# A four-mixer transformer stack in f32: first norm from rows, a clock guard, and two program parts recorded in turn

## The chip, the cores and the metric

The kernel runs on one core of one Trainium2 chip. The metric is device time in microseconds (us) of one execution, the median of several. Engines are named as the profile does: PE is TensorE (PEld its weight loads), DVE is VectorE, ACT is ScalarE, POOL is GpSimd, SP is the engine that issues most transfers. A "product" below is one matrix multiplication instruction of PE.

## The reference

A sequence of 512 rows of width 1024 passes four layers; each is a mixer and then a gated feed-forward part of hidden width 2816, both behind an RMS norm, and a last RMS norm closes the stack. Everything is float32.

```python
def rmsnorm(x, g):
    y = x * rsqrt(mean(square(x), -1) + 1e-5)
    return y * g

def rwkv7_mix(x, ...):                       # layer 0: 16 heads of 64
    xx = token_shift(x) - x
    xr, xw, xk, xv, xa, xg = (x + xx * mu[c] for c in range(6))
    r, k, v = xr @ w_r, xk @ w_k, xv @ w_v
    ...                                      # decay d, gates a and g, normalized key kk
    def step(state, t):                      # 512 steps of a 64 x 64 state per head
        sa = state @ kk_t
        state = state * d_t - outer(sa, kk_t * a_t) + outer(v_t, k_t)
        return state, state @ r_t
    ...                                      # group norm of y, a bonus term, gate, output product

h = x
for i, mix in enumerate((rwkv7_mix, swa_sink_mix, sgu_chunk_mix, gla_mix)):
    h = h + mix(rmsnorm(h, norm_mix[i]))
    h = h + (silu(n @ w_gate) * (n @ w_up)) @ w_out        # n = rmsnorm(h, norm_ffn[i])
return rmsnorm(h, norm_final)
```

The second mixer is attention in a window of 128 with a sink, the third a gated unit with chunks of 128, the fourth gated linear attention.

## The kernel before

The host passes x twice: `x`, with the 512 tokens in rows, and `x_t`, with the 1024 features in rows (eight tiles of 128 features x 512 tokens).

**The planner.** The code does not issue instructions directly: class `K` records operations into a `Program`, and `Program.run` (a list scheduler) issues them. Among the next `WINDOW` = 700 recorded operations it always takes the one that can start first by its own prices (`price`), and among equals the one recorded first. Recording order therefore sets priorities and which buffers are taken, but not alone the order on an engine. Each engine then executes its own instructions strictly in the order that was issued. All operations are recorded by one helper, so the profile gives the line L233 for all of them; groups are told apart by tile names.

**Fills.** The planner models PE's clock: it counts product columns per stretch of `TICK` = 3413 ns, and takes PE at half speed where the stretch before had less than `BUSY`. `keep_warm` puts products of the 128 x 128 identity with itself ("fills", their own line L448) where it expects PE to wait at least `GAP` = 450 ns. A fill writes to a PSUM bank that nobody reads.

**Weights.** A large product in f32 is split in three: `weights` loads a tile `wraw`, ACT copies it to a rounded `whi`, DVE (or, with `pool` true, POOL) subtracts to get `wlo`; `mm3` multiplies hi by hi, hi by lo and lo by hi.

**The mix stage** (`rwkv`). The first norm: ACT squares the eight tiles of `x_t`, DVE adds them up (`acc`), PE transposes, DVE reduces to one mean per token (`ms`), `rsqrt` makes `rcol` in ten small operations, PE broadcasts it along features by transposes, DVE copies it out of PSUM (`rbc`, a tile `slot`). Then, for each of the eight feature tiles, DVE multiplies `h` by gain and `rbc`, forms the shifted difference `xx`, and mixes; the products of the key follow with `rw_w_k`, whose `wlo` POOL makes for the first four tiles.

**The groups.** The sixteen heads are worked off in four groups. `ahead(n)` prepares group n: `rwkv_prepare` (elementwise, a scan `ew`, tiles `et`, `qk`), two halves of `rwkv_products` (`pa`, `pr`), `rwkv_inverse` (an inverse of 64 x 64 triangles by a ping-pong of products on PE and masked sums on DVE, tiles `mt` and `iv`; two parts), `rwkv_direct`. `rwkv_chain` then walks group n through the eight blocks of 64 tokens (four loops of two, the state in `st`, tiles `vu`, `wu`), with `rwkv_out` after every second loop (tiles `out`, `grs`, partly on POOL). The state makes the chain a strict sequence. In the program the whole of `ahead(n + 1)` is recorded, then the whole of chain n. `ahead(0)` comes first; the product of v (`gemm_tok`) fills the time beside it.

**Attention** (`swa`, `attend`): scores from 64-row products, the maximum on DVE (`mx`), exponentials on ACT, the scaling by POOL (`slot<-slot,smx`), transposes on PE, and products with the values; weight products of the neighbouring projections stand among them.

**The end** (`finish`, `store`): DVE multiplies the sums by the final gain, `rcol` is made for each half, ACT and DVE scale one half tile each, and SP issues eight transfers of 256 KB.

Of the kernel before, what the change touches and what calls it, by code (L numbers as in the profile page):

```python
# [29 lines left out]
ALSO = {"exp": ("tanh",), "sigmoid": ("tanh",), "silu": ("sin", "tanh"), "gelu": ("tanh",)}  # L30
ORDER = 1
EARLY = (("pa", 1), ("iv", 4), ("ew", 4))
# [157 lines left out]
class Program:  # L190
# [5 lines left out]
    FREE, GAP, TAIL, TURN = 4, 450.0, 150.0, 92.0  # L196
    TICK, BUSY = 10240 / 3, 3350.0

    def __init__(self, tc):
        self.tc, self.ops, self.last = tc, [], None  # L200
        nc = tc.nc
        self.tensor, self.vector, self.scalar = Engine(self, "PE", nc.tensor), Engine(self, "DVE", nc.vector), Engine(self, "ACT", nc.scalar)
        self.gpsimd, self.sync = Engine(self, "POOL", nc.gpsimd), Engine(self, "SP", nc.sync)
        self.cold, self.warm, self.fills, self.form = 0.0, None, 0, (P, P, 0)

    def pool(self, name, bufs, **kw):
# [81 lines left out]
    def run(self):  # L288
# [15 lines left out]
        while order < n:  # L304
# [40 lines left out]
            if e == "PE" and self.warm and op.ready > 0.0:  # L345
                now["PE"] = self.keep_warm(now["PE"], s, work)
                if now["PE"] > s:
                    continue
# [47 lines left out]
    def keep_warm(self, now, s, work):  # L396
# [7 lines left out]
        while True:  # L404
# [8 lines left out]
            now = t  # L413

    def count(self, work, span, t, cost, columns):
        n = int(t // span)
# [15 lines left out]
class K:  # L432
# [46 lines left out]
    def load_x(self, h):  # L479
        for k in range(KT):  # L480
            self.nc.sync.dma_start(h[k], self.d['x_t'][k * P:(k + 1) * P, :])

# [109 lines left out]
    def finish(self, half, nh):  # L592

        nc = self.nc
        c = slice(nh * S, nh * S + S)
        bs = (2 * half, 2 * half + 1)
        for b in bs:
            sq = self.slot()
            nc.scalar.activation(sq, self.h[b][:, c], AF.Square, accum_out=self.ss[:, 2 * b + nh:2 * b + nh + 1])
        if self.kind == 'final':  # L600
            for b in bs:
                nc.vector.tensor_mul(self.h[b][:, c], self.h[b][:, c], self.g[nh])
            return
# [71 lines left out]

    def rstd(self, acc=None):

        nc = self.nc
        if acc is None:
            col = self.rcol()  # L680
        else:
            ms, col = [self.sm.tile([P, NB], F32, name=n) for n in ("ms", "rcol")]
            ps = self.bank()
            for b in range(NB):
                nc.tensor.transpose(ps[:, b * P:(b + 1) * P], acc[:, b * P:(b + 1) * P], self.ident)
            nc.vector.tensor_reduce(ms, self.blocks(ps), axis=AX.X, op=ALU.add)
            nc.vector.tensor_scalar(ms, ms, 1.0 / D, EPS, op0=ALU.mult, op1=ALU.add)
            self.rsqrt(col, ms)
        ps = self.bank()
        for b in range(NB):  # L690
            nc.tensor.transpose(ps[:, b * P:(b + 1) * P], col[:, b:b + 1].to_broadcast([P, P]), self.ident)
        bc = self.slot()
        nc.vector.tensor_copy(bc, ps)
        return col, bc

# [220 lines left out]
    def rwkv(self, g, g_next, slots):  # L916
# [4 lines left out]

        nc, d, v = self.nc, self.d, self.v
        ex, inner, early, wide, tall = [ExitStack() for _ in range(5)]
# [10 lines left out]

        hn = self.h
        nc.vector.memset(keep, 1.0)
# [4 lines left out]
        acc = self.slot()  # L941
        for k in range(KT):
            t = acc if k == 0 else tp.tile([P, S], F32, name="t")
            nc.scalar.activation(t, hn[k], AF.Square)
            if k:
                nc.vector.tensor_add(acc, acc, t)
        _, rbc = self.rstd(acc=acc)
        xx = []
# [77 lines left out]
        def ahead(n):  # L1026
# [7 lines left out]
            subs.append(sb)  # L1034
            self.rwkv_prepare(sb, rf, kf, twa, keep, sel, rs, ka1)
            for hf in range(2):
                self.rwkv_products(sb, hf)
            self.rwkv_inverse(sb)
            self.rwkv_direct(sb)
        ahead(0)  # L1040
        for c in range(2):
# [48 lines left out]
    def rwkv_prepare(self, sb, rf, kf, twa, keep, sel, rs, ka1):  # L1090
# [18 lines left out]
        for i, p in enumerate(sb['pairs']):  # L1109
# [26 lines left out]
            nc.vector.tensor_mul(outer(qk), nat(rf[p]), nat(e))  # L1136
            sb['kn'].append(kn)
        ps = self.bank()
        for i in range(G):
# [26 lines left out]
    def rwkv_inverse(self, sb):  # L1166
# [29 lines left out]
        part = lambda t, r, j: t[r, j * 64:(j + 1) * 64]  # L1196
        sb['inv'] = []
        for k in range(2):
            zk = lambda r, j: z[r, k * 2048 + j * 256 + (64 if r.start else P):][:, :64]
# [3 lines left out]
            for lv in range(2):  # L1203
# [18 lines left out]
                u = u2  # L1222
            sb['inv'].append(u)

    def rwkv_direct(self, sb):
# [20 lines left out]
    def rwkv_chain(self, sb, tg):  # L1246
# [11 lines left out]
        for b in range(NB):  # L1258
# [46 lines left out]
            if b % 2:  # L1305
                self.rwkv_out(sb, b // 2, y, tg)

    def rwkv_out(self, sb, hf, y, tg):
# [460 lines left out]
def trace(prog, d, es, stages):  # L1769
    k = K(prog, d, es)  # L1770
    k.h = k.eight()
    k.load_x(k.h)
    k.v = k.load_cols()
    g_mix = lambda i: (lambda j: k.v['norm_mix'](i * KT + j))
# [42 lines left out]
```

## Time and profile before

| what | value |
|---|---|
| median of 3 runs | 2604.38 us (2601.57 to 2606.51) |
| the profiled execution's own time | 2596.65 us |
| its span | 2595.0 us, mean granted PE clock 0.994 |
| PE busy | 2517.9 us |
| DVE, ACT, POOL busy | 1802.4, 1314.1, 377.6 us |
| fills | 190 |
| first real product | 24.36 us |
| output products of the mix stage start | 461.28 us |

The span is that of one execution recorded by the profiler; the time beside it contains 1.65 us around the span. In a timeline row the columns are start, length, engine, line, operation, output and inputs, shape, count, and in brackets the engine's idle time ahead of it with what ended that. Adjacent alike instructions share a row. PE keeps two records of 0.27 us for one f32 fill, overlapped, so a count of 46 there is 23 fills. In a windows row the columns are the stretch, its length, busy time and instructions of PE, PEld, DVE, ACT and POOL, PE's granted clock (1.00 is full), the share of the transfer engines in use, and GB/s. A fill counts as busy PE.

### The profile page before, as it was taken

How to read it: one execution, taken by the hardware profiler on the slowest of the kernel's cores; microseconds unless marked ns; L12 is line 12 of the kernel's file. 1: busy time of each engine (PE TensorE's matmuls, PEld its weight loads, DVE VectorE, ACT ScalarE, POOL GpSimd, SP SyncE). 2: the span in 40 equal slices, each digit the busy share in tenths (PEclk: the TensorE clock that was granted, in tenths of full speed). 3: DMA queues.
4: the chain of work that ended last, by engine and by line, in shares of the span. 5: the costliest groups of instructions: out<-in, count | busy, mean ns of one | idle time of the engine just before them, and what ended most of it. 6: DMA issues, size and time to landing. Idle time of an engine off the chain costs nothing.

```text
span 2595.0 us, 37573 instructions
## 1 busy us (share of the span) xinstructions
PE 2517.9 (97%) x14378; PEld 2052.6 (79%) x14378; DVE 1802.4 (69%) x2804; ACT 1314.1 (51%) x2156; POOL 377.6 (15%) x521
## 2 busy tenths in 40 slices
PE   9999898999999989999999999999999999999998
PEld 8577777997888756988787888888878777888886
DVE  8685875487778863787776655577868634577868
ACT  4544454465646455656464333565556523565555
POOL 1000111022112232121221000012111000121111
PEclk9999999999999999999999999999999999999999
DMA  3220001489898412898985232389887221489885
GB/s 128 62 75 10 10 4 59 120 195 225 214 225 176 129 49 49 179 211 225 213 218 146 90 98 83 82 216 228 208 213 187 84 81 57 98 219 226 221 199 117
DMA packets 126004, 365.20 MB, mean 141 GB/s; under 512 B 13296, under 2 KB 19952, under 8 KB 125824
## 3 DMA queue, kind: packets, MB, share of 16 engines
q0 software_dynamic: 41472, 138.43, 29.8%
q1 hardware_dynamic: 84352, 224.37, 26.9%
q8 instruction: 113, 1.85, 0.3%
q14 instruction: 67, 0.55, 0.1%
HBM read 358.29 MB, written 2.10 MB: 139 GB/s over the span
## 4 chain that ended last, share of the span: by engine, by line
PE 47%; DMA 5%; issue 5%; DVE 4%; ACT 3%; POOL 0%; SPq 0%; ACTq 0%; POOLq 0%; DVEq 0%
PE ps L233 47%; DMA wraw<-ffn_w_b 3%; DVE slot L233 2%; ACT slot L233 2%; DMA wraw<-ffn_o_a 2%; DVE wlo L233 1%; ACT whi L233 1%; DMA wraw<-ffn_w_a 1%; DVE h L233 0%; POOL wraw L233 0%; DVE mx L233 0%; DMA slot<-slot 0%; SPq L233 0%; DVE left L233 0%; ACT left L233 0%
## 5 line engine op out<-in xcount | busy, mean ns | idle before, releaser
L233 PE MATMUL ps<-whi,slot 128*128 128x512 f32 (+1 forms) x5072 | 1557.7, 384 | 17.8 <-DVE slot L233 9.3
L233 PEld LDWEIGHTS ps<-whi,slot 128*128 128x128 f32 x5072 | 943.7, 188 | 199.5 <-issue 21.4
L233 DVE TENSOR_TENSOR wlo<-wraw,whi 128x1024 fp32r<-128x1024 f32 (+2 forms) x628 | 720.2, 1153 | 398.8 <-ACT whi L233 396.4
L233 ACT CAST whi<-wraw 128x1024 fp32r<-128x1024 f32 (+3 forms) x632 | 625.1, 993 | 732.2 <-PE ps L233 554.7
L233 PE MATMUL ps<-wlo,slot 128*128 128x512 f32 (+1 forms) x2536 | 969.1, 383 | 1.9 <-DVE wlo L233 1.7
L233 PEld LDWEIGHTS ps<-wlo,slot 128*128 128x128 f32 x2536 | 476.9, 188 | 86.1 <-DVE wlo L233 6.2
L233 PE MATMUL ps<-slot,whi 128*128 128x512 f32 (+2 forms) x864 | 275.8, 397 | 0.1
L233 DVE TENSOR_TENSOR slot<-ps,slot 128x512 f32<-128x512 f32 (+2 forms) x287 | 155.0, 566 | 91.0 <-PE ps L233 61.7
L233 PEld LDWEIGHTS ps<-slot,whi 128*128 128x128 f32 (+2 forms) x864 | 157.2, 185 | 48.3 <-issue 6.6
L233 POOL DMA_DIRECT2D wraw<-ffn_w_a x128 | 109.1, 853 | 512.5 <-DVE wlo L233 375.7
L233 PE MATMUL ps<-slot,wlo 128*128 128x512 f32 (+2 forms) x432 | 169.5, 393 | 0.8 <-DVE wlo L233 0.8
L233 POOL DMA_DIRECT2D wraw<-ffn_w_b x64 | 54.7, 859 | 772.7 <-DMA wraw<-ffn_w_b 517.8
L233 DVE TENSOR_TENSOR slot<-left,slot 128x512 fp32r<-128x512 f32 (+1 forms) x214 | 137.5, 661 | 34.3 <-ACT slot L233 28.8
L233 DVE TENSOR_TENSOR h<-h,ps 128x512 f32<-128x512 f32 x192 | 127.1, 683 | 29.8 <-PE ps L233 28.4
L233 ACT CAST slot<-left 128x512 fp32r<-128x512 f32 (+1 forms) x214 | 123.8, 598 | 34.3 <-PE ps L233 26.4
L233 PEld LDWEIGHTS ps<-ident,slot 128*128 128x128 f32 (+1 forms) x676 | 69.2, 141 | 41.9 <-POOL slot L233 14.4
L233 ACT COPY slot<-ps 128x512 f32<-128x512 f32 (+1 forms) x137 | 75.2, 563 | 50.8 <-PE ps L233 49.2
L233 PE MATMUL ps<-ident,slot 128*128 128x128 f32 (+1 forms) x676 | 89.4, 268 | 11.4 <-POOL slot L233 9.0
L233 PEld LDWEIGHTS ps<-slot,wlo 128*128 128x128 f32 (+2 forms) x432 | 79.6, 184 | 21.3 <-issue 3.3
L233 POOL DMA_DIRECT2D wraw<-ffn_o_a x64 | 54.5, 852 | 278.6 <-DVE wlo L233 204.9
L233 ACT COPY left<-ps 128x512 f32<-128x512 f32 x100 | 50.5, 555 | 54.7 <-PE ps L233 54.7
L233 DVE TENSOR_TENSOR slot<-slot 128x512 fp32r<-128x512 f32 (+9 forms) x93 | 62.0, 672 | 15.8 <-ACT slot L233 14.6
(278 smaller groups left out, 2267.3 us busy)
## 6 DMA issues: line engine op xcount, KB each, us to landing
wraw<-ffn_w_a SPq DMA_DIRECT2D x128, 512.0 KB, 6.5
wraw<-ffn_w_a POOLq DMA_DIRECT2D x128, 512.0 KB, 6.1
wraw<-ffn_o_a SPq DMA_DIRECT2D x64, 512.0 KB, 5.0
wraw<-ffn_o_a POOLq DMA_DIRECT2D x64, 512.0 KB, 8.0
wraw<-ffn_w_b SPq DMA_DIRECT2D x64, 384.0 KB, 3.3
wraw<-ffn_w_b POOLq DMA_DIRECT2D x64, 384.0 KB, 6.2
wraw<-ffn_o_b SPq DMA_DIRECT2D x16, 512.0 KB, 4.3
wraw<-ffn_o_b POOLq DMA_DIRECT2D x16, 512.0 KB, 7.7
```

Source lines behind the costliest of these rows:

```text
L233: op = self.add(eng.name, lambda: getattr(eng.target, what)(*map(real, args), **{k: real(a) for k, a in kw.items()}), *self.price(eng.name ...
```

## The change

It has five parts.

1. The first norm's mean squares come from `x` in rows (`token_squares`): eight half rows of 128 x 512 are loaded ahead of the weights, ACT squares six with an accumulated sum, DVE's bn_stats takes the two of the last 128 tokens. The eight adds, four transposes and the reduction go. `x_t` is loaded tile by tile in the key's loop. The broadcast is copied out of PSUM by ACT, and the first tile reads it from PSUM itself (`near`).
2. All of the key's `wlo` are made on DVE.
3. A guard in the planner (`ahead_of_cold`): if the last `TICK` before the end of the next product would hold less than `DENSE` = 3550 columns, a fill is put ahead of it, once that density has first been reached.
4. `ahead(n + 1)` and `rwkv_chain` are generators, recorded in turn by `ORDER`: five pieces of the preparation (two pairs of heads, two halves of products, the set-up of the inverse), then one loop of the chain and one piece of the preparation by turns.
5. The store: for the left halves one operation multiplies by the column and the gain; both halves are written in place, and four transfers of 512 KB write out whole rows.

```diff
-ORDER = 1
+ORDER = "pppppcpcpcpc"
...
+    TICK, BUSY, DENSE = 10240 / 3, 3350.0, 3550.0
...
                 now["PE"] = self.keep_warm(now["PE"], s, work)
-                if now["PE"] > s:
+                if now["PE"] > s or self.ahead_of_cold(now, s, op, work):
                     continue
...
+    def ahead_of_cold(self, now, s, op, work):
+        pool, call, first = self.warm
+        free = pool.slots["ps"].free
+        t, end = max(s, now["PE"]), s + op.cost
+        if not first.done or not free or min(free) + self.SEM > t:
+            return False
+        sum_ = op.columns
+        for b, e, c in reversed(self.recent):
+            if e <= end - self.TICK:
+                break
+            sum_ += c * (e - max(b, end - self.TICK)) / (e - b)
+        if sum_ >= self.DENSE:
+            self.armed = True
+            return False
+        if not self.armed:
+            return False
+        cost = 224.0 if work.get(int(t // self.TICK) - 1, 0.0) >= self.BUSY else 448.0
+        call()
+        self.fills += 1
...
+        now["PE"] = t + cost
+        return True
...
         if self.kind == 'final':
-            for b in bs:
-                nc.vector.tensor_mul(self.h[b][:, c], self.h[b][:, c], self.g[nh])
+            if nh:
+                for b in bs:
+                    nc.vector.tensor_mul(self.h[b][:, c], self.h[b][:, c], self.g[nh])
             return
...
+    def token_squares(self):
+        nc = self.nc
+        ss, ms = self.sm.tile([P, 2 * NB], F32, name="ss2"), self.sm.tile([P, NB], F32, name="ms")
+        st, mv = self.lay.tile([P, 2, 6], F32, name="xst"), self.lay.tile([P, 2], F32, name="xmv")
+        for j in range(2):
+            for b in range(NB):
+                x = self.slot()
+                nc.sync.dma_start(x, self.d['x'][b * P:(b + 1) * P, j * S:(j + 1) * S])
+                if b == NB - 1:
+                    nc.vector.bn_stats(st[:, j, :], x)
+                else:
+                    nc.scalar.activation(x, x, AF.Square, accum_out=ss[:, 2 * b + j:2 * b + j + 1])
+        nc.vector.bn_aggr(mv, st)
...
         bc = self.slot()
-        nc.vector.tensor_copy(bc, ps)
-        return col, bc
+        if ms is None:
+            nc.vector.tensor_copy(bc, ps)
+            return col, bc
+        nc.scalar.copy(bc, ps)
+        return ps, bc
...
         for k in range(KT):
-            nc.vector.scalar_tensor_tensor(hn[k], hn[k], g(k), rbc, op0=ALU.mult, op1=ALU.mult)
+            nc.sync.dma_start(hn[k], d['x_t'][k * P:(k + 1) * P, :])
+            nc.vector.scalar_tensor_tensor(hn[k], hn[k], g(k), rbc if k else near, op0=ALU.mult, op1=ALU.mult)
...
-            hi, lo = self.weights(d['rw_w_k'][k * P:(k + 1) * P, :], 1, D, k < 4)
+            hi, lo = self.weights(d['rw_w_k'][k * P:(k + 1) * P, :], 1, D)
...
-            if n < 3 and ORDER:
-                ahead(n + 1)
...
-            self.rwkv_chain(sb, tg)
-            if n < 3 and not ORDER:
-                ahead(n + 1)
+            chain, other = self.rwkv_chain(sb, tg), ahead(n + 1) if n < 3 else iter(())
+            for x in ORDER:
+                next(chain if x == "c" else other, None)
...
-                for nh in range(2):
-                    c = slice(nh * S, nh * S + S)
-                    o = self.slot()
-                    if nh:
-                        nc.scalar.activation(o, self.h[b][:, c], AF.Identity, scale=col[:, j:j + 1])
-                    else:
-                        nc.vector.tensor_scalar(o, self.h[b][:, c], col[:, j:j + 1], None, op0=ALU.mult)
-                    nc.sync.dma_start(self.d['out'][b * P:(b + 1) * P, c], o)
+                l, r = self.h[b][:, :S], self.h[b][:, S:]
+                nc.vector.scalar_tensor_tensor(l, l, col[:, j:j + 1], self.g[0], op0=ALU.mult, op1=ALU.mult)
+                nc.scalar.activation(r, r, AF.Identity, scale=col[:, j:j + 1])
+                nc.sync.dma_start(self.d['out'][b * P:(b + 1) * P, :], self.h[b])
```

A `yield` in the functions of the groups (two in `rwkv_prepare`, one per half in the loop of `rwkv_products`, after the set-up and after each part in `rwkv_inverse`, after each loop in `rwkv_chain`) is where one recording hands over to the other.

More of the change, by code (lines that the diff above doesn't have):

```diff
@@ L196 @@
     FREE, GAP, TAIL, TURN = 4, 450.0, 150.0, 92.0
-    TICK, BUSY = 10240 / 3, 3350.0
+    TICK, BUSY, DENSE = 10240 / 3, 3350.0, 3550.0
     def __init__(self, tc):
@@ L204, in __init__ @@
         self.cold, self.warm, self.fills, self.form = 0.0, None, 0, (P, P, 0)
+        self.recent, self.armed = [], False
     def pool(self, name, bufs, **kw):
@@ L413, in keep_warm @@
             now = t
+    def ahead_of_cold(self, now, s, op, work):
[17 more added lines that the diff above has]
+        self.fills += 1
+        self.form = P, P, 0
+        self.count(work, self.TICK, t, cost, 512.0)
+        now["PE"] = t + cost
+        return True
     def count(self, work, span, t, cost, columns):
+        self.recent.append((t, t + cost, columns))
+        if len(self.recent) > 400:
+            del self.recent[:200]
         n = int(t // span)
@@ L477, in eight @@
         return [t[k // 2][:, (k % 2) * S:(k % 2 + 1) * S] for k in range(KT)]
-    def load_x(self, h):
-        for k in range(KT):
-            self.nc.sync.dma_start(h[k], self.d['x_t'][k * P:(k + 1) * P, :])
     def load_h(self):
@@ L674, in rcol, with rstd @@
         return col
-    def rstd(self, acc=None):
+    def token_squares(self):
         nc = self.nc
-        if acc is None:
+        ss, ms = self.sm.tile([P, 2 * NB], F32, name="ss2"), self.sm.tile([P, NB], F32, name="ms")
[9 more added lines that the diff above has]
+        nc.vector.bn_aggr(mv, st)
+        s2 = ss.rearrange("p (b n) -> p b n", b=NB)
+        l = NB - 1
+        nc.vector.scalar_tensor_tensor(ms[:, l:], mv[:, 0:1], mv[:, 0:1], mv[:, 1:2], op0=ALU.mult, op1=ALU.add)
+        nc.vector.tensor_scalar(ms[:, l:], ms[:, l:], EPS, None, op0=ALU.add)
+        nc.vector.tensor_add(ms[:, :l], s2[:, :l, 0], s2[:, :l, 1])
+        nc.vector.tensor_scalar(ms[:, :l], ms[:, :l], 1.0 / D, EPS, op0=ALU.mult, op1=ALU.add)
+        return ms
+    def rstd(self, ms=None):
+        nc = self.nc
+        if ms is None:
             col = self.rcol()
         else:
[L682 to L687, printed above, removed]
+            col = self.sm.tile([P, NB], F32, name="rcol")
             self.rsqrt(col, ms)
@@ L692, in rstd @@
         bc = self.slot()
-        nc.vector.tensor_copy(bc, ps)
-        return col, bc
+        if ms is None:
+            nc.vector.tensor_copy(bc, ps)
+            return col, bc
+        nc.scalar.copy(bc, ps)
+        return ps, bc
     def operand(self):
@@ L916, in rwkv @@
     def rwkv(self, g, g_next, slots):
-        nc, d, v = self.nc, self.d, self.v
+        nc, d = self.nc, self.d
         ex, inner, early, wide, tall = [ExitStack() for _ in range(5)]
@@ L935, in rwkv @@
         hn = self.h
+        ms = self.token_squares()
+        v = self.v = self.load_cols()
         nc.vector.memset(keep, 1.0)
@@ L940, in rwkv @@
         nc.vector.memset(sel[64:, 15:16], 1.0)
[L941 to L947, printed above, removed]
+        near, rbc = self.rstd(ms)
         xx = []
@@ L1034, in ahead @@
             subs.append(sb)
-            self.rwkv_prepare(sb, rf, kf, twa, keep, sel, rs, ka1)
+            yield from self.rwkv_prepare(sb, rf, kf, twa, keep, sel, rs, ka1)
             for hf in range(2):
                 self.rwkv_products(sb, hf)
-            self.rwkv_inverse(sb)
+                yield
+            yield from self.rwkv_inverse(sb)
             self.rwkv_direct(sb)
-        ahead(0)
+            yield
+        for _ in ahead(0):
+            pass
         for c in range(2):
@@ L1051, in rwkv @@
             oo += sb['oo']
-            self.rwkv_chain(sb, tg)
-            if n < 3 and not ORDER:
-                ahead(n + 1)
+            chain, other = self.rwkv_chain(sb, tg), ahead(n + 1) if n < 3 else iter(())
+            for x in ORDER:
+                next(chain if x == "c" else other, None)
+            for x in chain:
+                pass
+            for x in other:
+                pass
         self.load_h()
@@ L1137, in rwkv_prepare @@
             sb['kn'].append(kn)
+            yield
         ps = self.bank()
@@ L1197, in rwkv_inverse @@
         sb['inv'] = []
+        yield
         for k in range(2):
@@ L1223, in rwkv_inverse @@
             sb['inv'].append(u)
+            yield
     def rwkv_direct(self, sb):
@@ L1306, in rwkv_chain @@
                 self.rwkv_out(sb, b // 2, y, tg)
+            yield
     def rwkv_out(self, sb, hf, y, tg):
@@ L1771, in trace @@
     k.h = k.eight()
-    k.load_x(k.h)
-    k.v = k.load_cols()
     g_mix = lambda i: (lambda j: k.v['norm_mix'](i * KT + j))
```

## The prediction

> **What bounds the kernel now.** I read the page's shares first, then the timeline of the start, of the recurrent groups, of the attention and of the end, and last the windows for clock and idle time.
>
> ```profile
> span 2595.0 us, 37573 instructions
> PE 2517.9 (97%) x14378; PEld 2052.6 (79%) x14378; DVE 1802.4 (69%) x2804; ACT 1314.1 (51%) x2156; POOL 377.6 (15%) x521
> ```
>
> TensorE is busy 97% of the span. What the change can win is the other 77 us, the fill products counted as busy, and products at half clock. The planner's instruction order differs from before's only in the mix stage with the recurrent groups (0 to about 500 us), in the attention (880 to 990 us) and in the store, so the sum has its terms there; elsewhere the instructions run in the same order. The profiled execution took 2596.65 us, 1.65 us outside its span, and is 7.7 us below the median 2604.38. I sum against it and carry the difference over to the median.
>
> **The start.** The order now is: eight squares, sum, transposes, one column, broadcast, first product.
>
> ```profile
> 7.42 2.67 ACT L233 ACTIVATE t<-h 128x512 f32<-128x512 f32 x4 [0.52 <-DMA h<-x_t]
> 11.54 0.68 DVE L233 TENSOR_TENSOR slot<-slot,t 128x512 f32<-128x512 f32 x1
> 12.23 4.67 POOL L233 TENSOR_TENSOR wlo<-wraw,whi 128x1024 fp32r<-128x1024 f32 x2 [10.86 <-ACT whi L233]
> 14.66 2.27 DVE L233 TENSOR_SCALAR rcol<-ms 128x4 int32<-128x4 int32 x1
> ...
> 19.30 5.30 PE L448 MATMUL ps<-ident 128*128 128x128 f32 x46
> 19.50 0.69 DVE L233 COPY slot<-ps 128x512 f32<-128x512 f32 x1 [0.81 <-PE ps L233]
> 20.23 1.41 DVE L233 SCALAR_TENSOR_TENSOR h<-h,vec,slot 128x512 f32<-128x512 f32 x2
> ...
> 24.36 1.76 PE L233 MATMUL ps<-slot,whi 128*128 128x512 f32 x6
> 28.73 0.75 DVE L233 SCALAR_TENSOR_TENSOR h<-h,vec,slot 128x512 f32<-128x512 f32 x1
> 31.24 2.39 POOL L233 TENSOR_TENSOR wlo<-wraw,whi 128x1024 fp32r<-128x1024 f32 x1 [14.34 <-ACT whi L233]
> 31.32 2.87 DVE L233 SCALAR_TENSOR_TENSOR h<-h,vec,slot 128x512 f32<-128x512 f32 x1
> ```
>
> The last square ends at 10.09, the sum at 12.22, the column at 18.70, and the first real product starts at 24.36. Fills hold the gap: 46 records are 23 products, 0.23 us each. The column's second operation took 2.27 us beside POOL's wlo; at the end of the kernel, with POOL still, the same one takes 0.17.
>
> ```profile
> 2581.21 0.17 DVE L233 TENSOR_SCALAR rcol<-ms 128x2 int32<-128x2 int32 x1
> L233 DVE BATCH_NORM_STATS2 st<-slot 128x6 f32<-128x512 f32 x16 | 10.5, 687 | 0.1
> 2579.08 1.22 DVE L233 TENSOR_TENSOR wlo<-wraw,whi 128x1024 fp32r<-128x1024 f32 x1
> ```
>
> After the change: the eight halves of x in rows land where x_t landed (the last square starts near 9.4 now). The last goes to DVE's bn_stats (0.69), to about 10.1; the small operations and two column copies end near 11.9, Newton's nine near 13.4. wlo is now DVE's at 1.22 and stands before the column's last operation: column 14.85. Four transposes end near 15.9, after the fills queued ahead of them. The first norm product reads PSUM directly and waits for no copy: 16.7. Then two differences, mix, cast, as now: first product about 19.8, 4.5 us earlier. Behind that, DVE is full from 25 to 50 us (25.00), and POOL's two later wlo stall it by some 2.1 us each; PE idles 0.78 us there.
>
> ```profile
> 25.00:50.00 25.00, 24.22 (x107) 19.48 (x106) 25.00 (x38) 8.69 (x13) 5.13 (x3) 1.00 0.18 57
> 175.00:200.00 25.00, 24.90 (x278) 20.88 (x278) 17.95 (x37) 7.16 (x10) 0.00 (x0) 1.00 0.16 49
> 200.00:222.00 22.00, 21.99 (x309) 17.57 (x310) 4.63 (x7) 5.06 (x10) 3.58 (x5) 1.00 0.05 15
> ```
>
> All four wlo go to DVE, 1.22 each, so little of the 0.78 is kept: 0.2. Start: −4.7. Ends: −2.5 (x in rows stands in SP's queue ahead of the weights and x_t: 2 MB more, 5.3 us at the 390 GB/s that the store reaches below, if a weight is late by half of it) and −6 (all idle there gone).
>
> **The guard.** Each guard fill costs 0.23 where TensorE has work waiting and nothing where it waits. The planner puts 9 in before the groups (175 to 222 us), where PE is full, with clock 1.00: +2.1, and no dip to save. In the groups 103 fills stand where 63 do.
>
> ```profile
> L448 PE MATMUL ps<-ident x126: 272/275/378, 234.2 to 419.6; 128*128 128x128 f32 x126
> 222.00:461.28 239.28, 218.33 (x3028) 179.29 (x3024) 167.71 (x355) 115.74 (x249) 36.27 (x126) 0.99 0.07 21
> 446.00:449.30 3.30, 1.48 (x13) 1.25 (x14) 1.59 (x5) 1.73 (x4) 1.10 (x6) 1.00 0.00 0
> 450.00:455.00 5.00, 4.96 (x43) 3.96 (x43) 1.83 (x4) 1.75 (x4) 1.40 (x7) 0.72 0.00 0
> 285.00:290.00 5.00, 4.33 (x62) 3.50 (x64) 4.84 (x6) 1.63 (x4) 2.77 (x4) 0.66 0.15 50
> ```
>
> A dip costs up to half of 3.4 us: 5 us at 0.66 lost 1.7. The one at 449 us followed a stretch in which PE was busy 1.48 of 3.30 us: a thin stretch is enough. The Trainium skill ("TensorE: Matmul & The Clock Gate", What's actually happening) has the half rate come after an idle window of about 3.4 us; this trace differs, 1.48 of 3.30 busy. By that rule neither dip in the groups would come from waits that the change can shorten, the 1.7 credited at 285 below would go, and the sum would be 1.7 higher.
>
> **The groups in turn.** Of 239.3 us PE idles 21.0 and fills 14.5 (63 times 0.23), so about 204 are real work, which stays.
>
> ```profile
> 272.39 5.30 PE L448 MATMUL ps<-ident 128*128 128x128 f32 x46
> 278.04 1.15 PE L233 MATMUL ps<-ident,mt 64*64 64x64 f32 x32 [0.35 <-DVE mt L233]
> 285.61 0.45 PE L233 MATMUL ps<-ident,out 128*128 128x128 f32 x1 [1.83 <-DVE out L233]
> 405.00:433.00 28.00, 24.99 (x556) 22.27 (x556) 16.81 (x28) 10.23 (x24) 4.75 (x18) 1.00 0.21 70
> L448 PE MATMUL ps<-ident x30: 272/276/377, 407.1 to 419.6; 128*128 128x128 f32 x30
> 461.28 9.65 PE L233 MATMUL ps<-et,rk 128*128 128x256 f32 x80
> L233 DVE TENSOR_TENSOR_SCAN ew<-keep,ew 128x512 f32<-128x512 f32 x6 | 8.1, 1356 | 0.6 <-ACT ew L233 0.6
> L233 DVE TENSOR_TENSOR ew<-ew,et 128x512 f32<-128x512 f32 x6 | 4.1, 684 | 0.0
> ```
>
> Cycle 1: with the alternation eight more DVE operations (a scan of 1.36, the rest near 0.7 or below) precede the first inverse's mt, about 4.5 us, and DVE, which runs in order, also waits 1.6 for chain 0's step: the inverse starts about 6 later, near 284, behind 49 fills (11.3 us) in the same wait. That phase then has less on DVE, and chain 0's last out, which PE waited 1.83 for, is already past, with its dip: −1.7. I take the next chain's start as +0. Cycle 2: 15 more fills (3.4) and 1.3 of the next group's products moved in, +4.7. Cycle 3: the third inverse overlaps the chain's last steps, which in before it followed, with 3.0 idle and 15 fills (3.5) from 405 to 433 us; about half goes: −3. The last chain, from there to 461.28, has the same order: 0. Sum +1.7, taken as +2. Ends: −3 (a third of the 21 idle gone and half of it given to fills) and +9 (the late inverse and all of cycle 2 kept).
>
> **The attention.** Guard fills change the order here: 9 and 7 stand ahead of the last scores, and the two gaps behind them are filled otherwise.
>
> ```profile
> 909.12 1.01 PE L233 MATMUL ps<-ident,slot 128*128 128x128 f32 x4 [4.25 <-POOL slot L233]
> 970.50 0.69 PE L233 MATMUL ps<-ident,slot 128*128 128x128 f32 x2 [4.71 <-POOL slot L233]
> 903.58 0.62 PE L233 MATMUL ps<-slot,whi 128*128 128x512 f32 x2
> 904.03 0.39 PE L233 MATMUL ps<-slot,wlo 128*128 128x512 f32 x1
> 910.00:920.00 10.00, 9.63 (x34) 4.53 (x33) 6.24 (x15) 7.79 (x29) 5.70 (x6) 0.83 0.18 52
> 970.00:980.00 10.00, 8.70 (x29) 4.17 (x30) 8.02 (x20) 9.64 (x39) 6.21 (x8) 0.75 0.00 0
> ```
>
> Ahead of the first transposes stand 27 weight products where 11 did, and 24 where 8 did: 16 times 0.225 (two steps in 0.45, from the rows) is 3.6 us of real work in each gap. Behind the last attention product 45 remain of 62, and 47 of 74. Against it: fills 9 and 7 times 0.23, and one wlo (1.22) now ahead of the first maximum, so the softmax is 1.0 to 1.4 later. First, where nine fills (2.1) and the later softmax run in one wait, so that the delay of the softmax counts: −3.8 (17 times 0.225) +1.3, and the dip behind the gap (10 us at 0.83, 1.7 lost) mostly gone, −1.4: −3.9. Second, where the fills may hold the scores themselves: −6.1 (27 times 0.225) +1.6 +1, and part of its dip (2.5 lost), −0.9: −4.4. Attention: −8.3, with ends −3 and −11. Behind it the feed-forward part's loads follow the buffers that PE frees, so it moves along.
>
> **The end.** Four of the eight multiplications by the gain are fused with the column's, and four stores of 512 KB replace eight of 256.
>
> ```profile
> 2587.16 4.47 SPq L233 DMA_DIRECT2D out<-slot  x8
> 2592.00:2593.00 1.00, 0.00 (x0) 0.00 (x0) 0.00 (x0) 0.00 (x0) 0.00 (x0) 0.50 1.04 385
> ```
>
> The column loses two multiplications ahead of it (near 0.7 each, as the sum's 0.68): −1.3. A store of 512 KB then waits for DVE and ACT both, one operation of each more (0.75 for the product with the gain, as 28.73 above, or 0.67 on ACT, as 7.42), and for a transfer whose first half is twice as long to fill: +1.1, while the queue was already full at a share of 1.04. −0.2, with ends −0.9 (one operation hidden) and +0.7.
>
> **The sum.** −4.7 + 2.1 + 2 − 8.3 − 0.2 = −9.1: 2587.5 beside 2596.65, and 2595.3 on the median. About 0.2%, 5.2 us, is what a measurement here can tell from no change.
>
> **The rivals.** Slower: the inverses stay late. Each needs DVE between its products (the timeline shows mt before nearly every one), and with the alternation DVE has both streams in one order. If the 6 us of the first inverse aren't regained and recur in all three cycles, the groups cost +18 in place of +2: 16 above the forecast, +6.9, 2611.3. It decides from +11 on there (net slower than before), and passes 0.2% from +16. For it: the wait of 0.35 for mt stands behind 23 fills, so this wait was really 5.7 long. Against it: DVE is busy 167.7 of 239.3 us, so it has room to catch up. Chance 0.2.
>
> No change: the attention gives nothing but the first gap's dip, since ACT is busy 9.64 of 10 us in the second one and may hold its end, so that the products pulled forward leave holes: −1.4 in place of −8.3, sum −2.2, 2602.2. Against it: 17 and 27 fewer products are left behind the last attention product, whatever sets that. Chance 0.17.
>
> Faster still: the alternation removes the idle time that it is laid against, 10 of 21, and fills there lie in waits: −8 in place of +2, sum −19, 2585. Chance 0.1; the third cycle's overlap speaks for it. My forecast's chance is 0.53.
>
> **How the numbers follow.** The forecast's own ends, with the terms unlikely to fail together, are 2588 to 2602. The range reaches to the faster rival and most of the slower: 2585 to 2611. Faster by over 0.2%: most of the forecast (0.48), the faster rival, and 0.04 of the second: 0.62. Within: 0.05, 0.12 of the second and 0.03 of the slower: 0.2. Slower: 0.18.
>
> **What would show it.** First real product near 19.8 us, no DVE operation of 2 us beside a POOL wlo; the groups' out projection starts near 461 us (461.28 − 4.7 + 2.1 + 2 = 460.7) with 103 fills before it; the two waits for POOL's slot shrink from 9.0 (4.25 and 4.71) to under 3 us; clock at 910 us near 1.00; the store's last 10 us as before. Wrong, if the out projection starts after 470, or if idle time appears behind the attention's transposes as large as the waits that went.

## The result, and the profile after

The changed kernel takes 2609.41 us (13 runs, 2606.82 to 2614.63) against 2599.07 of the kernel before (13 runs): ratio 1.0037, interval 1.0027 to 1.0048, so about 10 us slower. Forecast were 2595.3, and faster.

The page after; its first lines answer to those shown of before:

```profile
span 2606.8 us, 37773 instructions
PE 2550.0 (98%) x14482; PEld 2073.6 (80%) x14482; DVE 1796.5 (69%) x2801; ACT 1317.5 (51%) x2163; POOL 371.2 (14%) x517
```

PE is busy 32 us more, in a span 11.8 us longer, for the same products less four transposes, and 54 fills more (244 in place of 190). The timeline of the start:

```profile
15.75 0.60 PE L234 MATMUL ps<-ident,rcol 128*128 128x128 f32 x4
16.38 0.75 DVE L234 SCALAR_TENSOR_TENSOR h<-h,vec,ps 128x512 f32<-128x512 f32 x1 [1.03 <-PE ps L234]
19.95 2.25 PE L234 MATMUL ps<-slot,whi 128*128 128x512 f32 x8
```

The window from 25 to 50 us:

```profile
25.00:50.00 25.00, 25.00 (x112) 20.70 (x111) 24.98 (x41) 11.64 (x16) 0.00 (x0) 1.00 0.34 106
```

The first real product starts at 19.95 (24.36 before), and PE no longer waits from 25 to 50 us. Up to 100 us the changed kernel is 5.5 us ahead, at 145 us 5.1. Then all of it goes, and more. The timeline of the v stretch and of the start of the output products:

```profile
153.01 0.86 PE L234 MATMUL ps<-ident,h 128*128 128x128 f32 x4 [1.73 <-DVE h L234]
...
203.96 1.58 PE L478 MATMUL ps<-ident 128*128 128x128 f32 x6
...
474.21 9.42 PE L234 MATMUL ps<-et,rk 128*128 128x256 f32 x77
```

Windows of the v stretch and the groups, and then the line of all fills there, `keep_warm`'s and the guard's (two records for a fill, so 103 fills):

```profile
150.00:160.00 10.00, 8.27 (x36) 4.47 (x35) 9.93 (x20) 2.68 (x4) 0.00 (x0) 0.83 0.15 52
222.00:474.20 252.20, 242.98 (x3116) 194.95 (x3116) 166.66 (x352) 119.69 (x253) 38.76 (x126) 0.99 0.06 20
```
```profile
L478 PE MATMUL ps<-ident x206: 275/275/377, 236.9 to 448.6; 128*128 128x128 f32 x103
```

Three fills take 1.58 us at 204 us. In the groups PE idles only 9.2 us (252.20 less 242.98), where it idled 21.0, and still the output products start 12.9 us later. The idle time has been turned into fills, and the fills must be on the path, which the experiments test. In the attention, first the waits of PE from 900 to 1040 us (total, times, longest), then the timeline of PE and DVE, then two windows:

```profile
PE ps L234 <- POOL slot L234: 0.6, 1, 0.6
```
```profile
912.99 3.72 PE L478 MATMUL ps<-ident 128*128 128x128 f32 x14 [1.32 <-DVE slot L234]
917.36 1.22 PE L478 MATMUL ps<-ident 128*128 128x128 f32 x4
917.47 0.42 DVE L234 SCALAR_TENSOR_TENSOR slot<-ps,mask 128x256 f32<-128x256 f32 x1 [2.20 <-PE ps L234]
975.12 4.17 PE L478 MATMUL ps<-ident 128*128 128x128 f32 x14 [0.92 <-DVE slot L234]
```
```profile
910.00:920.00 10.00, 8.51 (x35) 6.32 (x37) 6.20 (x11) 0.00 (x0) 0.00 (x0) 0.72 0.84 297
975.00:985.00 10.00, 9.70 (x42) 7.76 (x43) 7.34 (x18) 1.49 (x8) 0.00 (x0) 0.66 0.14 39
```

The waits for POOL's slot did go, from 9.0 to 0.6. But nine fills (18 records) took 4.9 us and the next seven 4.2, most of them at half clock (granted 0.72 and 0.66 over these windows). They stand ahead of the last scores, and DVE waited 2.20 for those.

To see where the time went I paired the weight products of two traces by their count from the end, and took the difference of their starts. The table has this lag behind the kernel before (us) at five products, named by their time in before; then the PE time lost to half clock (the sum of one less the granted clock over windows of 1 us) in the groups (222 to 520 us) and around the attention (880 to 1130), and the fills from 222 to 480 us. A dash: not counted in whole fills.

| kernel | 145 | 516 | 800 | 1112 | 2583 | lost, groups | lost, attention | fills |
|---|---|---|---|---|---|---|---|---|
| before | 0 | 0 | 0 | 0 | 0 | 3.4 | 6.8 | 63 |
| changed | −5.1 | 13.3 | 13.2 | 11.5 | 12.2 | 1.7 | 6.8 | 103 |
| e1 | −5.0 | 11.3 | 10.8 | 8.5 | 11.9 | 6.8 | 6.8 | 66 |
| e2 | −5.7 | 21.3 | 22.2 | 25.3 | 26.4 | 3.4 | 10.3 | 129 |
| e3 | −5.7 | 8.6 | 8.2 | 5.0 | 4.7 | 13.7 | 8.5 | 46 |
| e4 | −4.9 | −5.1 | −3.3 | −12.7 | −14.4 | 5.1 | 6.8 | 54 |
| e5 | −5.2 | 3.3 | 4.8 | 8.0 | 9.9 | 3.4 | 15.4 | 94 |
| e6 | 1.6 | 17.2 | 17.8 | 11.5 | 12.0 | 18.8 | 10.2 | 46 |
| e7 | 0.1 | −0.2 | −1.0 | −7.4 | −5.4 | 6.8 | 3.4 | 67 |
| e8 | −3.9 | −5.3 | −3.0 | −15.8 | −18.6 | 8.5 | 3.4 | 54 |
| e9 | −4.4 | −6.0 | −3.5 | −6.0 | −7.3 | 6.8 | 5.1 | 54 |
| e10 | −5.9 | 11.1 | 13.8 | 3.6 | 2.3 | 1.7 | 5.1 | 103 |
| e11 | −5.3 | 20.1 | 21.3 | 18.8 | 21.2 | 0.0 | 10.2 | − |
| e12 | −1.8 | 5.7 | 7.3 | −6.8 | −10.3 | 11.9 | 3.4 | 71 |
| e13 | −5.6 | 8.2 | 8.5 | 4.7 | 11.7 | 3.4 | 6.8 | − |

The changed kernel thus won 5.1 by 145 us, lost 18.4 up to 516, and won 1.7 in the attention where 8.3 were forecast. The table's columns are those of one execution; the medians stand with each run. The granted clock is on record for every execution: one less it, times the span, is what half clock took from the whole of it, to about 1 us. At the median over the runs that is 18 us for the kernel before, for the changed one, for e4 and for e13, but 31 for e3, 35 for e6, 25 for e5 and 13 for e7. So the changed kernel's 10 us are not lost to half clock.

### The profile page after: what moved, and what is told of

It is laid out like the page before. It is cut to its first block, busy times and chain, and to the rows that moved or that the text cites. A ratio compares the mean times of both kernels' runs of the same rounds, so it can differ in the third digit from the quotient of the medians.

```text
span 2606.8 us, 37773 instructions
## 1 busy us (share of the span) xinstructions
PE 2550.0 (98%) x14482; PEld 2073.6 (80%) x14482; DVE 1796.5 (69%) x2801; ACT 1317.5 (51%) x2163; POOL 371.2 (14%) x517
## 4 chain that ended last, share of the span: by engine, by line
PE 50%; DMA 5%; DVE 4%; issue 3%; ACT 2%; POOL 0%; SPq 0%; DVEq 0%; POOLq 0%; ACTq 0%
PE ps L234 50%; DMA wraw<-ffn_w_b 3%; DMA wraw<-ffn_o_a 2%; DVE slot L234 2%; ACT slot L234 1%; ACT whi L234 1%; DVE wlo L234 1%; DMA wraw<-ffn_w_a 1%; DVE h L234 0%; PE ps L478 0%; DVE mx L234 0%; POOL wraw L234 0%; DMA slot<-slot 0%; POOL slot L234 0%; SPq L234 0%
## 5 line engine op out<-in xcount | busy, mean ns | idle before, releaser
L234 PE MATMUL ps<-whi,slot 128*128 128x512 f32 (+1 forms) x5072 | 1556.0, 384 | 18.6 <-DVE h L234 8.2
L234 ACT CAST slot<-left 128x512 fp32r<-128x512 f32 (+1 forms) x214 | 123.9, 599 | 32.8 <-PE ps L234 26.4
L234 PEld LDWEIGHTS ps<-ident,slot 128*128 128x128 f32 (+2 forms) x672 | 67.8, 139 | 30.5 <-issue 7.5
L234 PE MATMUL ps<-ident,slot 128*128 128x128 f32 (+2 forms) x672 | 87.4, 265 | 2.9 <-DVE slot L234 2.1
L478 PE MATMUL ps<-ident 128*128 128x128 f32 x488 | 80.9, 302 | 4.4 <-DVE slot L234 2.2
```

What stands on the lines that cost most here:

```text
L234: op = self.add(eng.name, lambda: getattr(eng.target, what)(*map(real, args), **{k: real(a) for k, a in kw.items()}), *self.price(eng.name ...
L478: self.nc.tensor.target.matmul(self.ps.tile_pool.tile([P, S], F32, name="ps")[:, :P], self.ident.real(), self.ident.real(), start=True, st ...
```

## The experiments

**e1, no guard.** In `run`:

```diff
-                if now["PE"] > s or self.ahead_of_cold(now, s, op, work):
+                if now["PE"] > s:
```

> The changed kernel with the guard off (the alternation, the first norm from rows and the store stay). In the profile of the changed kernel, against the one of before, the start has gained 5.5 us, the stretch of the v product and the inverse of group 0 has lost 6.8, the groups have lost another 11.6 by the output products (461.3 to 474.2), the attention has gained 1.2. Theory G, the guard: its fills stand in PE's own order in front of products that are needed, and the recurrent groups are late mostly by them. Then without it the output products start near 460 (461.3 - 5.5 + 4), and the time is about 3 us under before. Theory A, the alternation: the groups are late because both streams stand in one order on DVE. Then only the 6.8 us of the v stretch go, the output products start near 467, and the time is some 4 us over before.

2605.65 us, 1.0030 of before (1.0016 to 1.0043). The loss of the v stretch is gone, as both theories had it (the first chain starts at 221.9, in before at 226.9), but the lag grows by 16.3 us from 145 to 516, with 66 fills and 6.8 us lost to half clock. The time, 6.4 over before, is nearer to theory A's 4, and yet these groups lose more than theory A gives to the alternation.

**e2, in sequence.** The guard without the alternation:

```diff
-ORDER = "pppppcpcpcpc"
+ORDER = "pppppppp"
```

> The changed kernel with preparation and chain recorded one after the other as before (guard, first norm and store stay). Theory G: the groups stay late, output products at 467 or later, and the time is 3 to 6 us over before. Theory A: the groups' 11.6 us go, output products near 462 (the start's gain eaten by the 6.8 us of the v stretch), and the time is 1 to 2 us under before.

2622.39 us, 1.0098 (1.0080 to 1.0116): 23 us over before, where theory G had 3 to 6. With the guard in, recording in sequence takes 13 us more than in turn. Theory A falls: it isn't the alternation that made the changed kernel late. Theory G has the sign and not the size, and e1 shows that taking the guard out doesn't bring the time back.

**e3, start and store alone** (both edits above).

> The changed kernel without guard and without alternation: what is left is the first norm from rows, wlo on DVE and the store. Both theories: the start's 5.5 us arrive at the end, output products at 455.8, attention as before, the store 0.4 earlier: 5.9 us under before (ratio 0.9977). If the gain of the start is lost somewhere on the way (a transfer or a clock dip that falls otherwise), the time is within 2 us of before.

2605.39 us, 1.0022 (1.0012 to 1.0033): 6 us over before, and both expected times missed. The start is 5.7 ahead at 145 us and 8.6 behind at 516. Two windows of the groups show where it went:

```profile
360.00:390.00 30.00, 23.14 (x149) 16.38 (x150) 24.54 (x50) 11.56 (x22) 4.71 (x13) 0.72 0.00 1
430.00:450.00 20.00, 14.57 (x125) 11.64 (x124) 7.60 (x15) 8.87 (x22) 3.17 (x16) 0.74 0.16 54
```

Half clock took 13.7 us in the groups of this execution (3.4 before), and 13 us more than before over all runs (31 against 18). Nothing in the groups' program had been changed, but the planner's clock now stands elsewhere when it plans them: it put 46 fills where there had been 63, in another order. So a re-plan by itself is a suspect, and e1 stands under the same doubt.

**e4, the silent guard.** It plans as in the changed kernel, and keeps the order on all engines, but issues no fill:

```diff
         cost = 224.0 if work.get(int(t // self.TICK) - 1, 0.0) >= self.BUSY else 448.0
-        call()
-        self.fills += 1
```

> The changed kernel in which the guard plans its 53 or so fills and keeps the order that follows from them, but the fills themselves are not issued (they write to a bank that nobody reads, so the result is the same). It tells the fills' own time from the order that they bring about. Theory G with the fills' own time as its cost (53 fills at 0.23 to 0.45 us, most of them on PE's path): 12 to 20 us under the changed kernel, thus 2 to 10 under before, and the attention gains about 6 more (its 9 and 7 fills go while the products pulled forward stay). Theory G with the order as its cost: as late as the changed kernel in the groups, 3 to 5 us better at most. Theory A: 5 us under the changed kernel, most of it in the v stretch and in the attention.

2581.96 us, 0.9934 (0.9922 to 0.9947): 27.5 us under the changed kernel and faster than both. This is theory G, with the fills' own time as the cost, and more of it than the 12 to 20 us expected: 76 fills fewer (244 less 168; some 53 were expected), 0.36 us each. e2 and e5 below are a second such pair, with one plan in sequence: there 73 fills (284 less 211) cost 21.3 us, 0.29 each. The output products start at 455.74, which is 461.28 less the start's gain, so the alternation and the order together cost nothing in this plan; and the attention wins 9.4 from 800 to 1112. Its window of the groups, its fills there, and its timeline; the last fence is the changed kernel's timeline:

```profile
222.00:455.70 233.70, 216.28 (x2995) 176.34 (x2992) 165.89 (x352) 116.16 (x246) 38.62 (x126) 0.98 0.07 21
```
```profile
L476 PE MATMUL ps<-ident x108: 274/275/378, 232.8 to 292.3; 128*128 128x128 f32 x108
```
```profile
269.28 9.99 PE L476 MATMUL ps<-ident 128*128 128x128 f32 x88
...
348.29 1.15 PE L234 MATMUL ps<-mt 64*64 64x64 f32 x32
349.37 0.71 PE L234 MATMUL ps<-st,qk 128*128 128x128 f32 x4
```
```profile
274.05 9.99 PE L478 MATMUL ps<-ident 128*128 128x128 f32 x88
...
361.15 0.68 PE L234 MATMUL ps<-mt 64*64 64x64 f32 x14
361.75 0.49 PE L478 MATMUL ps<-ident 128*128 128x128 f32 x2
362.17 0.33 PE L234 MATMUL ps<-mt 64*64 64x64 f32 x2
362.43 0.49 PE L478 MATMUL ps<-ident 128*128 128x128 f32 x2
362.84 0.68 PE L234 MATMUL ps<-mt 64*64 64x64 f32 x16
363.45 0.71 PE L234 MATMUL ps<-st,qk 128*128 128x128 f32 x4
```

The same 44 fills (88 records of 9.99 us) stand ahead of the first inverse in both: `keep_warm` put them where it expected a wait, and e4, which issues them too, has lost nothing when the output products start. The guard's fills are the others. They break up the row of 32 records: 1.08 us from its start to the next row without fills (349.37 less 348.29), 2.30 with two (363.45 less 361.15). That is 0.61 for a fill. It is the dearest case: over the six rows of 32 `mt` products that hold fills in these groups, a fill took 0.39 to 0.61, and 0.39 where two stand together (at 421 us), which fits one change of shape for both.

**e5 to e8: how much is luck of the plan?** e5 is the silent guard in sequence, e6 and e7 are the kernel before with a shifted planner's clock, e8 the silent guard with the shift of e6 (e7 has 1100.0 in place of 400.0):

```diff
-        now = {e: 0.0 for e in ("PE", "DVE", "ACT", "POOL", "SP", "")}
+        now = {e: 400.0 for e in ("PE", "DVE", "ACT", "POOL", "SP", "")}
```

> The silent guard (planned, fills not issued) with preparation and chain recorded in sequence. With the alternation the silent guard came to 0.9934 of before, and its groups lost nothing (output products at 455.7, against 461.3 - 5.5). Theory A2, the alternation itself is worth its idle time once no fills stand in the way: in sequence the output products start 5 to 10 us later than 455.7, the time is 2587 to 2592. Theory R, the groups' length comes from how the plan happens to fall against the clock's dips, and neither order is better: any time from 2575 to 2605, and the difference lies in a few dips.

> The kernel before, with nothing changed but the planner's clock, which starts at 0.4 us in place of 0: the same operations and prices, but its stretches of 3.41 us fall elsewhere, and with them fills and order. Theory R, a re-plan alone moves the time by as much as the changes at stake: more than 4 us away from before, either way, with the difference in the groups and the attention. Rival, the plan is robust: within 2 us of before.

> As the run before, with the planner's clock started at 1.1 us. Theory R: again another time, more than 4 us from before or from the shift by 0.4 us. Rival: within 2 us of before.

> The changed kernel with the silent guard, and the planner's clock started at 0.4 us. If the silent guard's gain comes from what it does to every plan (products are kept back for the gaps), it stays: 2578 to 2588. Theory R, it was one lucky plan: it falls back to 2592 or more.

e5: 2601.09, 1.0000 (0.9986 to 1.0014). e6: 2608.73, 1.0026 (1.0012 to 1.0039). e7: 2590.91, 0.9951 (0.9933 to 0.9969). e8: 2581.23, 0.9923 (0.9898 to 0.9947). Theory R holds for the kernel before: the same program, planned from 0.4 or 1.1 us, moves by +8 or −10 us (medians), as much as the whole change. The windows of e6's groups show how:

```profile
222.00:478.00 256.00, 227.87 (x2996) 184.80 (x2995) 168.25 (x355) 119.06 (x252) 37.96 (x126) 0.93 0.06 20
360.00:410.00 50.00, 40.02 (x330) 29.20 (x330) 35.12 (x79) 23.08 (x47) 5.80 (x18) 0.80 0.01 4
```

18.8 us are lost to half clock there, and its output products start at 477.86. e7 wins in the attention alone, with 3.4 lost in place of 6.8. The silent guard with the alternation kept its gain in its second plan. e5 is 19 us over e4 (by the traces 24): it is 8.4 us later at 516 us, within the 5 to 10 that theory A2 had, and loses another 12.6 in the attention, with 15.4 at half clock, which A2 had not. That is one plan each, and the plans of the kernel before lie 18 us apart, so what the alternation is worth by itself is not shown.

**e9 and e10: which fills.** The silent guard, with the fills issued on one side of 700 us of the plan only:

```diff
-        call()
+        if t > 700e3:
+            call()
```

(e10 with `<`.)

> The changed kernel's plan, with the guard's fills issued in the attention only (16 of 76). In the changed kernel the attention gained 1.2 to 1.7 us on before, with the same order and no fills 8.5. If the fills themselves take that gain (they run at half clock ahead of the last scores and hold up DVE's masks), this run is 7 us over the silent guard (2589), all of it in the attention, and its groups are as in the silent one (output products at 455.7). If the attention's time falls by chance with the clock's stretches, the groups are the same but the attention is anything from 10 us better than before to 5 worse.

> The other half: the guard's fills issued in the v stretch and the groups only (60 of 76). Fills on PE's path: output products at 474, 18 us behind the silent guard, and the attention gains the 8.5 us again: 2601 to 2603. If the fills in the groups were hidden in waits, output products would stand near 457, and the time near 2584.

e9: 2589.28, 0.9958 (0.9943 to 0.9972). e10: 2601.74, 1.0009 (1.0000 to 1.0018). Both came out as expected, with output products from 455.10 and from 472.00: 16 fills in the attention cost 7.3 us (0.46 each, most of them at half clock), 60 ahead of it 19.8 (0.33 each). Together that is 27.1 of the 27.5. e10 wins 10.2 in the attention, e9 2.5.

**e11 and e13: what makes a fill dear.** All guard fills are issued; behind a product of 64 x 64 they are several of that shape in place of one of 128 x 128 (six in e11, shown here, and `range(2)` in e13; 39 fills):

```diff
-        call()
+        (self.small if self.form[:2] == (64, 64) else call)()
...
+        def small():
+            ps = self.ps.tile_pool.tile([P, S], F32, name="ps")
+            for j in range(6):
+                self.nc.tensor.target.matmul(ps[:64, j * 64:(j + 1) * 64], self.ident.real()[:64, :64], self.ident.real()[:64, :64], start=True, stop=True)
```

> The changed kernel with all its guard fills, in the same order, but behind a product of 64 x 64 a fill is six products of 64 x 64 with about the same time (six at 0.034 us, from a row of 32 in 1.08) in place of one of 128 x 128. In the changed kernel a row of 32 such products that takes 1.08 us took 2.30 with two fills within it: 0.61 for each, 0.23 for the product and 0.38 for the change of shape there and back. If the change of shape is the cost, some 39 fills save up to 0.38 each: 10 to 15 us under the changed kernel, output products near 460 to 464. If it is not (a fill's place in the order, a wait for its bank), the time stays within 3 us of the changed kernel.

> The run with small fills again, with two products of 64 x 64 in place of six behind a product of 64 x 64 (39 fills, same order). In the run with six, a row of products that took 1.08 us with no fill and 2.30 with two fills of 128 x 128 took 2.47 with two fills of six: 0.70 each, which is 12 records at 0.058, their own time and nothing beside it; my 0.034 for a product was wrong, as products of 64 rows that alternate between the two halves of the array overlap and these do not. If the change of shape is what makes a fill of 128 x 128 cost 0.61 in place of 0.23, two small ones (four records, 0.23) cost 0.23: 39 times 0.38 is 15 us, so 2592 to 2598 against 2609 of the changed kernel, output products near 460, and the row of 32 takes 1.55. If a fill costs its 0.4 beyond its product for another reason (the row that it breaks up), the time stays within 4 us of the changed kernel.

e11: 2616.99, 1.0064 (1.0049 to 1.0078), a miss, 7.6 us over the changed kernel where 10 to 15 under were expected: 0.034 for a product was wrong, as e13's expectation says. e13: 2600.87, 1.0000 (0.9990 to 1.0010), 8.5 us under the changed kernel where 11 to 17 were expected; the output products start at 469.04 and not near 460. The row of 32 in e13:

```profile
359.53 0.68 PE L234 MATMUL ps<-mt 64*64 64x64 f32 x14
360.04 0.22 PE L484 MATMUL ps<-ident 64*64 64x64 f32 x1
...
361.07 0.71 PE L234 MATMUL ps<-st,qk 128*128 128x128 f32 x4
```

It takes 1.54 with two fills: 0.23 each, as expected. So in this row 0.38 of the 0.61 goes with the change of shape there and back. The sum came short of 15 us, and one reason is in the trace: 10 of the 39 small fills have a fill of 128 x 128 right behind them, so that the shape changes all the same. 29 times 0.38 is 11.0. What is missing from there to 8.5 stays open; half clock doesn't account for it, as the granted clock has the same median over the runs of e13 and of the changed kernel (0.993). The traced execution of e13 took 2608.03, the highest of its twelve, so its row in the table stands above the median.

**e12, a third plan of the silent guard**, clock started at 1.1 us.

> The silent guard with the alternation in a third plan (planner's clock started at 1.1 us). The two plans so far came to 0.9934 and 0.9923 of before, while the kernel before ranged from 0.9951 to 1.0026 over its plans. If the silent guard with the alternation is better by itself: 2576 to 2590. If two plans were lucky: over 2592.

2588.52, 0.9953 (0.9935 to 0.9971): within the expected range, and the slowest of the three, with 11.9 us lost to half clock in the groups.

## Why the prediction was wrong

**Start: right.** First product at 19.8 forecast, 19.95 measured; −4.7 forecast, −5.1 to −5.5 measured. What I missed is that the gain needn't arrive: in e3, where the planner laid the groups out anew, it was gone by 516 us. I had compared orders, and priced only the differences that I could name.

**Guard: the failed step.** "Each guard fill costs 0.23 where TensorE has work waiting and nothing where it waits." 0.23 holds inside a run of fills, from which I had taken it. Between products of 64 x 64 one measured 0.39 to 0.61, in the attention, most of it at half clock, 0.46, and over all 76 it was 0.36: 27.5 us. The planner's own price has a part of this: it charges 92 ns for a change of shape (`TURN`), which my 0.23 leaves out. The v stretch shows the cost: 2.1 were forecast for 9 fills; from 145 to 227 us 6.4 were lost, of which e4, without the fills, lost 2.2 (both have a dip there, 1.7 in the changed kernel at 153 us), so that 4.2 are left for 11 fills.

**Groups: mechanism half right, size wrong.** +2 forecast, +18.4 from 145 to 516 us with the v stretch (4.1 forecast). The working of the +2 has a gap of its own: with cycle 1 at −1.7, its terms add up to 0, and +1.7 only with that −1.7 left out. I let the fills of the groups lie in the waits, 49 of them in that ahead of the first inverse. 44 did lie there; but they were `keep_warm`'s, and of the guard's many stood within the inverses' rows. The alternation and the new order, charged with 1.3 beside the fills in the second cycle, cost nothing together in e4. My slower rival came near by luck, with 2611.3 against 2609.41, and had the wrong cause: in the same order without the fills (e4) the loss is gone, so it is the fills in PE's order and not DVE's order of both streams. The first inverse, forecast 6 us late, came 9.4 late in the changed kernel and 4.6 in e4 (287.44 and 282.65 against 278.04).

**Attention: the order right, the fills wrong.** −8.3 forecast, −1.7 measured, and −9.4 in e4 with the same order. The step that failed is that nine fills and the later softmax run "in one wait": the fills stood in PE's order ahead of the last scores, so the softmax waited for them, most of the time at half clock. For the second gap I had allowed for fills that hold the scores, but at 1.6 us for seven, which took 4.2.

**The end: right**, −0.2 forecast and −0.35 measured (11.41 us from the last product to the end of the span before, 11.06 after).

**The signs.** Of the signs named in advance, the first product, the 103 fills and the shrunken waits for POOL's slot came in; the clock at 910 us did not (0.72 from 910 to 920 us, not near 1.00). And the one that was to show the forecast wrong did: the output products, by their first long row as in the forecast, start after 470, at 474.21 (the first single one at 469.20, before at 460.27).

**The clock's dips.** The dip at 153 us comes with a wait of 1.73 us, and the losses to half clock come in pieces of about 1.7 us (1.7, 3.4, 5.1, 6.8). The Trainium skill ("TensorE: Matmul & The Clock Gate", What's actually happening) has half clock come after an idle window of about 3.4 us. This trace differs, as no wait of 3.4 us stands at 153; the pieces of 1.7 agree with its windows of 3.4 us at half rate. By that rule the guard's fills would save nothing. In the groups of e4, with the same order and without them, 5.1 us were lost to half clock, in the changed kernel 1.7, so they did save, 3.4 us in these two executions. But from 222 to 516 us the changed kernel lost 12.0 and e4 won 2.4: the fills cost 14.4 us there, with that saving already counted.

## What to carry to other kernels

A filler on an in-order engine is free only inside a wait that has been seen in a trace; between products of another shape it cost here up to 0.61 us in place of 0.23, so price it from the neighbours that it will have and not from a run of its like. Where a planner writes the order, shift its clock by a few tenths of a microsecond before you believe a change of half a per cent: here the unchanged program spans 18 us over three plans. Separate what a planning rule does to the order from what it issues: here the same plan with nothing issued turned a loss of 10 us into a gain of 17.

## What I had not expected of the hardware

I had not expected how much the clock's dips vary with the plan: over the executions in the table, the groups lose between 0 and 18.8 us of PE time to half clock, and e6, the kernel before with its planner's clock shifted by 0.4 us, loses 35 us in a whole execution at the median where before loses 18. The silent guard with the alternation (e4, e8, e12: 0.9934, 0.9923, 0.9953 of before) is better than both kernels in each of three plans. Why the planned but silent fills lead to a better order (products kept back for the gaps, as seen in the attention, or fewer fills by `keep_warm`) I didn't separate further. e5, silent and in sequence, did not gain, and neither did e1, with the alternation and without the guard; but each of them is one plan.
